# Banks emptied by ScalarE alone, memory values in rows of 512 columns, and transposes of x in pairs, in a two-layer decoder trunk

## The chip, the cores and the metric

The kernel runs on one core of one Trainium2 chip. The metric is the device time of one execution in microseconds (us), as the median of three runs. The engines are TensorE (PE, matmuls), VectorE (DVE), ScalarE (ACT), GpSimd (POOL) and SyncE (SP), which here issues the DMAs.

## What is computed

Two layers of a decoder trunk over 512 tokens of 1024 channels. Each layer projects x once, feeds four gated branches of width 512 (an RWKV-7 recurrence, latent attention, a convolution module, cross-attention into 256 memory tokens), merges them, projects, and normalises. Cut to what the change touches:

```python
h = x @ W_in                       # split among the branches
# B: latent attention, 8 heads
q = (rms_norm(q_lat, q_norm) @ w_uq).reshape(B, S, H, 96)
kv = (rms_norm(kv_lat, kv_norm) @ w_ukv).reshape(B, S, H, 128)
# C: convolution module
y = depthwise_conv31(a * sigmoid(b)); y = silu(layer_norm(y))
# M: cross-attention into the memory
k, v = split(mem @ w_mem_kv)       # 256 memory tokens, 512 columns each
# end of a layer
x = layer_norm(alpha * x + merged @ w_out)
```

## The kernel before

All large matmuls are in float32 accuracy, made of three products: each operand is split into a rounded high part `h` and a rest `lo` (`split`: ScalarE copies to `h`, VectorE subtracts to get `lo`), and `mm3` issues three matmuls per 128 rows. Activations lie with channels on the partitions, 512 tokens in the columns; a PSUM bank holds 128 x 512 values.

Weights stream through SBUF: SyncE loads one raw block of 512 KB after the other into two buffers, each is split (`w25h`, `w25l` and so on, numbered in the order of use), and the split parts have three buffers. `stream` takes the work items in order and prefetches up to four blocks.

The order of the instructions on each engine is fixed when the program is built. A class `Plan` runs the work items and side tasks as generators, keeps a modelled clock for every engine, and at each step lets the task go on whose inputs are due. `plan.due` tells it when a task's inputs are ready, `yield` hands over, `plan.spawn` starts a side task. So an edit in one task can move instructions of others.

PSUM has three pools. `pp` has two banks, used by every projection (`project`, through which also `pq`, `pk` of the attention heads, `ps_xq`, `ps_mk` pass, and the narrow items `pz`, `pmv`); `pa` has two, used by transposes and small products (`ct`, `cb` of the convolution, `xT` of x); `pg` has four.

Touched parts:

- `heads` takes a scaled projection bank (`pq` or `pk`, two heads) and makes the two parts `xqh`, `xql` (or `xkh`, `xkl`); DMAs then put them in place. ScalarE and VectorE both read the bank.
- `conv_norm` transposes the convolution's result (`ct`), takes statistics and normalises into `cn`, and transposes back (`cb`), from where `ctn` (tanh) and `yc` (affine) are made.
- `memory_items` gives four key items (each 24 matmuls, bank `ps_mk`) and two value items (`vpart`, through `narrow`: two blocks of 128 x 256, bank `pmv`) per layer.
- At the end of layer 0, z (the sum before the last normalisation) comes from `out_item` (half z0) and quarter items (z2, z3). `norm` normalises the tokens; behind the fourth token block it transposes x for layer 1, `xT0` to `xT7`, one bank at a time, into `xf` and its parts `xh`, `xl`.
- `ORDER` (line 26) is the list, written by hand, in which those items and layer 1's memory items are put in the stream: m0 to m3 are keys, m4 and m5 values.

Of the kernel before, what the change touches and what calls it, by code (L numbers as in the profile page):

```python
# [10 lines left out]
F32 = mybir.dt.float32  # L11
F32R = mybir.dt.float32r
# [3 lines left out]
AF = mybir.ActivationFunctionType  # L16
ALU = mybir.AluOpType
# [5 lines left out]
SEQ = 512  # L23
DM = 1024
U_SLOTS = 32
ORDER = ["z0", "m0", "m1", "z2", "m2", "m4", "z3", "m3", "m5"]
LOOK = 4
GATHER = 1500.0
WR = 2
# [236 lines left out]
def trunk_kernel(ctx: ExitStack, tc: tile.TileContext, A, out, dbg=None):  # L266
    nc = tc.nc
    plan = Plan(tc.keep_in_program_order)
# [19 lines left out]
    def TR(o, i):  # L288
        plan.shape(128, 128)
        plan.op("PE", 109.0, _names(o), _names(i))  # L290
        plan.keep(nc.tensor.transpose(o, i, ident))  # L291
# [12 lines left out]
    xp = pool(8, name="xp")  # L304
# [194 lines left out]
    def wide(get, ps, lhs, wait=None):  # L499

        for k in range(8):
            h, lo = yield from get()
            if wait:
                yield from wait(k)
            for b in range(len(ps)):
                xh, xl = lhs(k, b)
                mm3(ps[b], xh, xl, h, lo, k == 0, k == 7)
                if b % 2 and (k < 7 or b < 3):
# [34 lines left out]
    closed = [False] * LAYERS  # L543
# [8 lines left out]
    def close_phase():  # L552
        phase[0].close()

    def memory_items(l):

        ms = []
        res = {}

        def load(pool):  # L560
            raws = []
            for i in range(4):
                raws.append(u(f"mr{i}_{l}"))
# [12 lines left out]
        def keep(x, i, b, ps):  # L576
            h, lo = (y[:, 256 * b:256 * b + 256] for y in res[x][i])
            return split(h, lo, ps)

        def keys(h):  # L580
            def run(get):
                ps = yield from project(get, ms, f"mk{h}_{l}", 256)
                yield from keep("k", h // 2, h % 2, ps)
                yield
            return run

        def vpart(b):
            def after(i, ps):
                yield from keep("v", i, b, ps)
                if b == i == 1:  # L590
                    MEM[l] = (res["k"], res["v"])
                yield

            def run(get):
                return narrow(get, 256, 2, f"pmv{b}{l}", lambda k, i: [x[:, 128 * i:128 * i + 128] for x in ms[k]], after)
            return run

        its = [([(A["w_mk"][l, h], (512, 512))], keys(h)) for h in range(4)]
        its += [([(A["w_mv"][l, b, kh], (512, 512)) for kh in range(2)], vpart(b)) for b in range(2)]
        return load, its, lambda: len(ms) == 8  # L600

    def layer_items(l):
# [4 lines left out]
        def pr(n, i=0, w=1):  # L607
            return PRM[l][0][:, PCOL[n] + i:PCOL[n] + i + w]
# [540 lines left out]
        def conv_norm():  # L1149
            ntok = []  # L1150
            yield lambda: added[3] == 8
            for tb in range(4):
                ps, = yield from pa.take([128, 512], f"ct{tb}" + t_)
                for i in range(4):
                    TR(ps[:, 128 * i:128 * i + 128], cacc[i][:, 128 * tb:128 * tb + 128])
                yield
                bs, mv = st(f"cbs{tb}" + t_, 6), st(f"cmv{tb}" + t_, 2)
                V.bn_stats(bs, ps)
                V.bn_aggr(mv, bs)
                rs = st(f"crs{tb}" + t_, 1)  # L1160
                rstd_of(rs, mv[:, 1:2], 1.0, LN_EPS)
                n = u(f"cn{tb}" + t_)
                V.tensor_scalar(out=n, in0=ps, scalar1=mv[:, 0:1], scalar2=rs, op0=ALU.subtract, op1=ALU.mult)
                pa.free()
                ntok.append(n)
                yield
            yield lambda: added[1] >= 4
            for i in range(4):
                ps, = yield from pa.take([128, 512], f"cb{i}" + t_)
                plan.due(*ntok)  # L1170
                yield "pe"
                for tb in range(4):
                    TR(ps[:, 128 * tb:128 * tb + 128], ntok[tb][:, 128 * i:128 * i + 128])
                yield
# [458 lines left out]
        def end_items():  # L1633
# [148 lines left out]
            def norm(tb):  # L1782
# [29 lines left out]
                if E["n"] < 4:  # L1812
                    return
                for k in range(8):
                    ps, = yield from pa.take([128, 512], f"xT{k}" + t_)
                    plan.due(*[z[tb][k // 4] for tb in range(4)])
                    yield
                    for tb in range(4):
                        TR(ps[:, 128 * tb:128 * tb + 128], z[tb][k // 4][:, 128 * (k % 4):128 * (k % 4) + 128])
                    yield  # L1820
                    f = u(f"xf{k}" + t_)
                    h = xp.tile([128, 512], F32R, tag="xh", name=f"xh{k}_{l + 1}")
                    lo = xp.tile([128, 512], F32R, tag="xl", name=f"xl{k}_{l + 1}")
                    S.activation(f, ps, AF.Identity, scale=pr("ln_g", k), bias=pr("ln_b", k))
                    pa.free()
                    S.copy(h, f)
                    V.tensor_tensor(out=lo, in0=f, in1=h.bitcast(F32), op=ALU.subtract)
                    X[l + 1].append((h, lo))
                close_phase()
                closed[l] = True  # L1830

            if l + 1 < LAYERS:
                load, its, there = memory_items(l + 1)
# [135 lines left out]
def layout(x, mem, positions, w_in, b_gate, rwkv_mu, rwkv_w0, rwkv_w2, rwkv_a0, rwkv_a2, rwkv_k_k, rwkv_k_a,  # L1969
# [30 lines left out]
    a["w_mv"] = np.stack([tiles(xattn_w_mem_kv[l][:, 512:], 256, 4) for l in range(L)])  # L2000
# [35 lines left out]
```

## Time and profile before

| | |
|---|---|
| median of 3 runs | 1505.58 us (1505.47 to 1506.05) |
| profiled execution | 1506.66 us |
| its span | 1504.9 us |
| mean granted TensorE clock | 0.996 |
| busy: PE, PE weight load, DVE, ACT, POOL | 1474.2, 1239.7, 1053.5, 662.1, 137.1 us |
| matmuls | 11896 |

The profiler takes one execution; its own time is 1.8 us more than its span. Busy time is that in which the engine executes; matmuls are pipelined, so a busy TensorE may still be waited on. A row such as `PE pq L286 <- DVE xql L235` says that a matmul into `pq` waited for VectorE's `xql`. L235 and L286 are helper lines, which all operations of an engine share, so that names of tiles and not lines tell the operations apart.

### The profile page before, as it was taken

The page shows a single profiled execution, that of the slowest core. Times are in us where ns is not written, and L with a number is a line of the kernel's source. Part 1 is how long each engine was busy: PE and PEld are TensorE (multiplying, and loading weights), DVE is VectorE, ACT ScalarE, POOL GpSimd, SP SyncE. Part 2 cuts the span into 40 slices and gives each one's busy share as a digit, 9 for nine tenths or more (in the row PEclk, how much of TensorE's full clock was granted, in tenths as well). Part 3 has the DMA queues.
Part 4 walks back from the last instruction along what each step waited for, and adds up shares of the span by engine and source line. Part 5 has one row for each costly group of instructions (what it writes and reads, how often), then busy time and mean ns, then how long its engine had stood idle before and what let it go on. Part 6 is the DMA issues. An engine that isn't in the chain of part 4 may idle for free.

```text
span 1504.9 us, 29132 instructions
## 1 busy us (share of the span) xinstructions
PE 1474.2 (98%) x11896; PEld 1239.7 (82%) x11896; DVE 1053.5 (70%) x1994; ACT 662.1 (44%) x1270; POOL 137.1 (9%) x329
## 2 busy tenths in 40 slices
PE   8999999999999999999999999999999999999997
PEld 8888878888888888888998878888887788888886
DVE  5799997755757666645554888887876476757747
ACT  5546554434354543443255455533444344444332
POOL 0000000030303030000010000000030203021002
PEclk9999999999999999999999999999999999999998
DMA  6444333241322323434343252423332313233532
GB/s 213 124 136 108 86 100 96 84 111 59 86 83 78 91 74 95 136 103 129 114 147 108 82 138 68 116 92 99 88 95 72 97 47 107 63 107 116 165 99 70
DMA packets 89013, 153.50 MB, mean 102 GB/s; under 512 B 41008, under 2 KB 47152, under 8 KB 88880
## 3 DMA queue, kind: packets, MB, share of 16 engines
q1 hardware_dynamic: 88880, 151.65, 33.9%
q8 instruction: 93, 1.52, 0.4%
q14 instruction: 40, 0.33, 0.1%
HBM read 134.32 MB, written 5.77 MB: 93 GB/s over the span
## 4 chain that ended last, share of the span: by engine, by line
PE 90%; DVE 5%; ACT 2%; issue 1%; DMA 1%; POOL 0%; SPq 0%; ACTq 0%; POOLq 0%; DVEq 0%
PE ps_m L286 23%; PE po L286 11%; PE ps_xq L286 3%; PE ps_v L286 3%; PE ps_xg L286 3%; PE ps_cg L286 3%; PE ps_rg L286 3%; PE ps_k L286 3%; PE ps_mg L286 3%; PE ps_r L286 3%; PE ps_val L286 3%; PE ps_glu L286 2%; PE ms L286 2%; PE pl L286 2%; PE pz L286 2%; PE pmv L286 2%
## 5 line engine op out<-in xcount | busy, mean ns | idle before, releaser
L235 DVE SCALAR_TENSOR_TENSOR cacc<-hpad,prm,cacc 128x512 f32<-128x512 f32 x240 | 179.2, 749 | 3.9
L235 ACT ACTIVATE tm<-ps_m,prm 128x512 f32<-128x512 f32 x64 | 44.1, 689 | 166.6 <-PE ps_m L286 156.1
L235 DVE SCALAR_TENSOR_TENSOR mt<-tm,po 128x512 f32<-128x512 f32 x48 | 32.9, 686 | 89.9 <-PE po L286 89.6
L235 POOL TENSOR_TENSOR tmpW<-ZT,W 64x14 f32<-64x14 f32 (+6 forms) x112 | 42.7, 381 | 7.8
L235 POOL TENSOR_TENSOR ZT<-ZT,tmpW 64x14 f32<-64x14 f32 (+6 forms) x112 | 42.0, 375 | 8.8
L235 ACT ACTIVATE mP<-ms,nmm 128x128 f32<-128x128 f32 (+3 forms) x64 | 33.6, 529 | 20.3 <-DVE nmm L235 19.5
L235 POOL TENSOR_SCALAR ZT<-W 64x256 f32<-64x256 f32 x8 | 3.6, 447 | 369.7 <-DMA W<-scr 369.7
L235 ACT COPY mPT<-mt 128x128 f32<-128x128 f32 (+3 forms) x64 | 26.1, 428 | 19.6 <-PE mt L291 19.4
L235 DVE TENSOR_TENSOR merged<-merged,mt 128x512 f32<-128x512 f32 x48 | 33.6, 699 | 1.7
L235 POOL MEMSET D<- 128x8 f32 x8 | 0.9, 116 | 342.7 <-PE ms L286 321.2
L235 DVE TENSOR_REDUCE nmm<-ms 128x1 f32<-128x128 f32 (+3 forms) x64 | 30.0, 484 | 0.1
L235 POOL TENSOR_SCALAR lrs<-lmv 128x1 f32<-128x1 f32 x8 | 3.6, 447 | 253.6 <-DVE lmv L235 252.2
L235 DVE TENSOR_SCALAR mP<-mP,smm 128x128 f32<-128x128 f32 (+3 forms) x64 | 24.8, 387 | 2.3
L291 PE MATMUL mt<-cst,mP 128*128 128x128 f32 x160 | 25.9, 273 | 0.0
L235 DVE SCALAR_TENSOR_TENSOR merged<-tm,po 128x512 f32<-128x512 f32 x16 | 11.0, 687 | 20.1 <-PE po L286 20.0
L235 ACT ACTIVATE z<-z,lnb,lrs 128x256 f32<-128x256 f32 (+1 forms) x16 | 9.6, 647 | 30.1 <-DVE lnb L235 30.1
L235 POOL TENSOR_SCALAR gr<-gm 128x8 f32<-128x8 f32 x8 | 2.4, 298 | 224.0 <-DVE gm L235 224.0
L235 ACT ACTIVATE yb<-yb,mr,gr 128x64 f32<-128x64 f32 x64 | 22.1, 434 | 1.1 <-DVE mr L235 1.1
L286 PE MATMUL ms<-kTl,qT 96*128 96x128 f32 (+3 forms) x64 | 22.3, 348 | 0.0
L291 PEld LDWEIGHTS mt<-cst,mP 128*128 128x128 f32 x160 | 19.0, 141 | 3.6 <-ACT xP L235 0.2
L235 ACT ACTIVATE xP<-xs,nmx 128x256 f32<-128x256 f32 x32 | 15.1, 473 | 13.7 <-DVE nmx L235 11.2
L286 PE MATMUL ms<-kTh,qT 96*128 96x128 f32 (+3 forms) x64 | 20.6, 322 | 0.0
(3536 smaller groups left out, 5276.3 us busy)
## 6 DMA issues: line engine op xcount, KB each, us to landing
w<-in_w_ch_dram SPq DMA_DIRECT2D x146, 512.0 KB, 3.8
w<-in_w_o_dram SPq DMA_DIRECT2D x32, 512.0 KB, 3.7
w<-in_w_out_dram SPq DMA_DIRECT2D x16, 512.0 KB, 3.7
w<-in_w_lat_dram SPq DMA_DIRECT2D x16, 336.0 KB, 3.2
w<-in_w_mk_dram SPq DMA_DIRECT2D x8, 512.0 KB, 3.7
w<-in_w_mv_dram SPq DMA_DIRECT2D x8, 512.0 KB, 3.7
w<-in_w_qk_dram SPq DMA_DIRECT2D x8, 320.0 KB, 2.9
x<-in_xT_dram SPq DMA_DIRECT2D x8, 256.0 KB, 5.9
```

Source lines behind the costliest of these rows:

```text
L235: return self.plan.keep(f(*a, **k))
L286: plan.keep(nc.tensor.matmul(o, lhsT, rhs, start=start, stop=stop))
L291: plan.keep(nc.tensor.transpose(o, i, ident))
```

## The change

Four edits:

1. In `heads` ScalarE copies the scaled bank to SBUF (in the tile of `lo`), and `split` makes both parts from there; VectorE no longer reads the bank. Eight copies more a layer on ScalarE.
2. In `conv_norm` ScalarE copies `ct` to SBUF and the bank is free; statistics and normalisation read the copy. The affine part of `yc` goes from VectorE to ScalarE.
3. A layer's memory values are one item through `wide`, with 48 matmuls of 512 columns in place of 96 of 256. In layer 1 it takes both `pp` banks, in layer 0 one `pp` and one `pa`. The weights `w_mv` are laid out for it, and in `ORDER` all of it stands behind z3 and m3, while before m4 stood ahead of z3.
4. The transposes of x are eight side tasks (`features`), so that both `pa` banks are in use at once.

```diff
-ORDER = ["z0", "m0", "m1", "z2", "m2", "m4", "z3", "m3", "m5"]
+ORDER = ["z0", "m0", "m1", "z2", "m2", "z3", "m3", "m4"]
...
-        def vpart(b):
-            def after(i, ps):
-                yield from keep("v", i, b, ps)
...
-                return narrow(get, 256, 2, f"pmv{b}{l}", lambda k, i: [x[:, 128 * i:128 * i + 128] for x in ms[k]], after)
+        def values(get):
+            ps = [pp.tile([128, 512], F32, tag="pp", name=f"pmv{i}_{l}") for i in range(1 + (l > 0))]
+            if l == 0:
+                ps += yield from pa.take([128, 512], f"pmv1_{l}")
+            yield from wide(get, ps, lambda k, b: [x[:, 128 * b:128 * b + 128] for x in ms[k]])
...
+            plan.spawn(after())
...
-        its += [([(A["w_mv"][l, b, kh], (512, 512)) for kh in range(2)], vpart(b)) for b in range(2)]
+        its += [([(A["w_mv"][l, i], (512, 512)) for i in range(4)], values)]
...
+                n = u(f"cn{tb}" + t_)
+                S.copy(n, ps)
+                pa.free()
                 bs, mv = st(f"cbs{tb}" + t_, 6), st(f"cmv{tb}" + t_, 2)
-                V.bn_stats(bs, ps)
+                V.bn_stats(bs, n)
...
-                V.tensor_scalar(out=n, in0=ps, scalar1=mv[:, 0:1], scalar2=rs, op0=ALU.subtract, op1=ALU.mult)
-                pa.free()
+                plan.due(rs)
+                yield
+                V.tensor_scalar(out=n, in0=n, scalar1=mv[:, 0:1], scalar2=rs, op0=ALU.subtract, op1=ALU.mult)
...
-                V.tensor_scalar(out=z, in0=ps, scalar1=pr("cln_g", i), scalar2=pr("cln_b", i), op0=ALU.mult, op1=ALU.add)
+                S.activation(z, ps, AF.Identity, scale=pr("cln_g", i), bias=pr("cln_b", i))
...
-            S.activation(parts[0], ps, AF.Copy, scale=s)
-            V.scalar_tensor_tensor(out=parts[1], in0=ps, scalar=s, in1=parts[0].bitcast(F32), op0=ALU.mult, op1=ALU.subtract)
+            raw = parts[1].bitcast(F32)
+            S.activation(raw, ps, AF.Copy, scale=s)
+            yield from split(*parts, raw)
...
                 for k in range(8):
-                    ps, = yield from pa.take([128, 512], f"xT{k}" + t_)
...
+                    plan.spawn(features(k, [z[tb][k // 4][:, 128 * (k % 4):128 * (k % 4) + 128] for tb in range(4)]))
```

What it does to the order. First, ScalarE in layer 0, at the first two pairs of attention heads (`pq`, `pk` are banks, `w25h` a weight's high part, `ps_xq` the bank of the projection that follows). Before:

```order
L235 COPY w25h<-w_1193 128x1024
L235 ACTIVATE xqh_1223<-pq_0_1203 128x512
L235 ACTIVATE xkh_1232<-pk_0_1219 128x512
L235 COPY w26h<-w_1230 128x1024
L235 ACTIVATE xqh_1272<-pq_0_1244 128x512
L235 ACTIVATE xkh_1283<-pk_0_1268 128x512
L235 ACTIVATE xqh_0_1324<-ps_xq_0_1280 128x512
```

After:

```order
L235 COPY w25h<-w_1139 128x1024
L235 ACTIVATE xql_1169<-pq_0_1149 128x512
L235 COPY xqh_1168<-xql_1169 128x512
L235 ACTIVATE xkl_1180<-pk_0_1164 128x512
L235 COPY xkh_1179<-xkl_1180 128x512
L235 ACTIVATE xql_1213<-pq_0_1191 128x512
L235 COPY xqh_1212<-xql_1213 128x512
L235 COPY w26h<-w_1177 128x1024
L235 ACTIVATE xkl_1234<-pk_0_1208 128x512
L235 COPY xkh_1233<-xkl_1234 128x512
L235 ACTIVATE xqh_0_1274<-ps_xq_0_1230 128x512
```

Each bank is read by one ScalarE instruction, `xql` or `xkl`, which writes the raw values; the high part is a second copy from SBUF behind it.

Second, TensorE at the end of layer 0, where layer 1's keys (`ps_mk`), its values (`pmv`) and the transposes of x (`xT`) meet. Before:

```order
L286 MATMUL ps_mk_1_8406<-memh_1_7798,w124l 128x256
L286 MATMUL pmv_8443<-w125l,memh_1_7792 128x256
L286 MATMUL pmv_8443<-w125h,memh_1_7792 128x256
L286 MATMUL pmv_8443<-w125h,meml_1_7793 128x256
...
L291 MATMUL xT_0_8434<-cst,z_0_7314 128x128
L286 MATMUL pmv_8443<-w125l,memh_1_7794 128x256
...
L291 MATMUL xT_0_8464<-cst,z_0_7314 128x128
L286 MATMUL pmv_8443<-w126l,memh_1_7796 128x256
```

After:

```order
L286 MATMUL ps_mk_1_8298<-memh_1_7756,w122l 128x256
L286 MATMUL pmv_1_8334<-w123l,memh_1_7750 128x512
L286 MATMUL pmv_1_8334<-w123h,memh_1_7750 128x512
L286 MATMUL pmv_1_8334<-w123h,meml_1_7751 128x512
L286 MATMUL pmv_1_8335<-w123l,memh_1_7750 128x512
...
L291 MATMUL xT_0_8344<-cst,z_0_7272 128x128
L291 MATMUL xT_0_8345<-cst,z_0_7266 128x128
...
L291 MATMUL xT_0_8345<-cst,z_0_7272 128x128
L286 MATMUL pmv_1_8334<-w123l,memh_1_7750 128x512
```

The second bank of the values is opened at once, and two groups of transposes stand side by side; before, one group stood between pieces of six value matmuls.

ScalarE at the same place (`z` is the normalisation of the last token block, `kmh` the high part of the keys, `xf` and `xh` what is made of a transposed bank). Before:

```order
L235 ACTIVATE z_0_7314<-z_0_7314,lnb_0_8430,lrs_0_8400 128x512
L235 COPY kmh_1_7802<-ps_mk_1_8406 128x256
L235 ACTIVATE xf_0_8458<-xT_0_8434,prm_194 128x512
L235 COPY xh_1_8459<-xf_0_8458 128x512
L235 COPY w126h<-w_8407 128x1024
L235 ACTIVATE xf_0_8479<-xT_0_8464,prm_194 128x512
```

After:

```order
L235 ACTIVATE z_0_7272<-z_0_7272,lnb_0_8322,lrs_0_8292 128x512
L235 COPY kmh_1_7760<-ps_mk_1_8298 128x256
L235 COPY w124h<-w_8299 128x1024
L235 ACTIVATE xf_0_8359<-xT_0_8344,prm_194 128x512
L235 COPY xh_1_8360<-xf_0_8359 128x512
L235 ACTIVATE xf_0_8364<-xT_0_8345,prm_194 128x512
```

The split of the values' next weight now stands ahead of the first copy out of the transposes. SyncE issues that weight's load, in both programs, behind the four stores of `xtok`.

Third, ScalarE in layer 1, at the first two pairs of heads (`yxg0h` and `xP` belong to the cross-attention). Before:

```order
L235 COPY w147h<-w_9552 128x1024
L235 ACTIVATE xqh_9585<-pq_1_9565 128x512
L235 COPY w148h<-w_9602 128x1024
L235 ACTIVATE xkh_9607<-pk_1_9581 128x512
L235 COPY yxg0h_9623<-xy_1_9266 128x512
L235 ACTIVATE xP_1_9589,smx_1_9597<-xs_1_9578,nmx_1_9596 128x256
L235 ACTIVATE xqh_9653<-pq_1_9619 128x512
```

After:

```order
L235 ACTIVATE xql_9490<-pq_1_9469 128x512
L235 COPY xqh_9489<-xql_9490 128x512
L235 COPY w148h<-w_9507 128x1024
L235 ACTIVATE xkl_9513<-pk_1_9485 128x512
L235 COPY xkh_9512<-xkl_9513 128x512
L235 COPY yxg0h_9528<-xy_1_9170 128x512
L235 ACTIVATE xP_1_9493,smx_1_9502<-xs_1_9482,nmx_1_9501 128x256
L235 ACTIVATE xql_9549<-pq_1_9524 128x512
```

Two copies more stand between the readings of the two `pq` banks.

More of the change, by code (lines that the diff above doesn't have):

```diff
@@ L507, in wide @@
                 mm3(ps[b], xh, xl, h, lo, k == 0, k == 7)
-                if b % 2 and (k < 7 or b < 3):
+                if b % 2 and (k < 7 or b < len(ps) - 1):
                     yield
@@ L574, in load, with keep @@
                     ms.append((h[:, c], lo[:, c]))
-        def keep(x, i, b, ps):
-            h, lo = (y[:, 256 * b:256 * b + 256] for y in res[x][i])
+        def keep(x, i, c, ps):
+            h, lo = (y[:, c] for y in res[x][i])
             return split(h, lo, ps)
@@ L582, in run, with after @@
                 ps = yield from project(get, ms, f"mk{h}_{l}", 256)
-                yield from keep("k", h // 2, h % 2, ps)
+                yield from keep("k", h // 2, slice(256 * (h % 2), 256 * (h % 2) + 256), ps)
                 yield
             return run
-        def vpart(b):
-            def after(i, ps):
-                yield from keep("v", i, b, ps)
[L590 to L594, printed above, removed]
-                return narrow(get, 256, 2, f"pmv{b}{l}", lambda k, i: [x[:, 128 * i:128 * i + 128] for x in ms[k]], after)
-            return run
+        def values(get):
[3 more added lines that the diff above has]
+            yield from wide(get, ps, lambda k, b: [x[:, 128 * b:128 * b + 128] for x in ms[k]])
+            def after():
+                for i in range(2):
+                    yield from keep("v", i, slice(0, 512), ps[i])
+                if l == 0:
+                    pa.free()
+                MEM[l] = (res["k"], res["v"])
+            plan.spawn(after())
+            yield
         its = [([(A["w_mk"][l, h], (512, 512))], keys(h)) for h in range(4)]
-        its += [([(A["w_mv"][l, b, kh], (512, 512)) for kh in range(2)], vpart(b)) for b in range(2)]
+        its += [([(A["w_mv"][l, i], (512, 512)) for i in range(4)], values)]
         return load, its, lambda: len(ms) == 8
@@ L1156, in conv_norm @@
                 yield
+                n = u(f"cn{tb}" + t_)
+                S.copy(n, ps)
+                pa.free()
                 bs, mv = st(f"cbs{tb}" + t_, 6), st(f"cmv{tb}" + t_, 2)
-                V.bn_stats(bs, ps)
+                V.bn_stats(bs, n)
                 V.bn_aggr(mv, bs)
@@ L1161, in conv_norm @@
                 rstd_of(rs, mv[:, 1:2], 1.0, LN_EPS)
-                n = u(f"cn{tb}" + t_)
-                V.tensor_scalar(out=n, in0=ps, scalar1=mv[:, 0:1], scalar2=rs, op0=ALU.subtract, op1=ALU.mult)
-                pa.free()
+                plan.due(rs)
+                yield
+                V.tensor_scalar(out=n, in0=n, scalar1=mv[:, 0:1], scalar2=rs, op0=ALU.subtract, op1=ALU.mult)
                 ntok.append(n)
@@ L1814, in norm, with features @@
                 for k in range(8):
-                    ps, = yield from pa.take([128, 512], f"xT{k}" + t_)
[L1816 to L1830, printed above, removed]
+                    plan.spawn(features(k, [z[tb][k // 4][:, 128 * (k % 4):128 * (k % 4) + 128] for tb in range(4)]))
+            def features(k, zs):
+                ps, = yield from pa.take([128, 512], f"xT{k}" + t_)
+                plan.due(*zs)
+                yield
+                for tb in range(4):
+                    TR(ps[:, 128 * tb:128 * tb + 128], zs[tb])
+                yield
+                f = u(f"xf{k}" + t_)
+                h = xp.tile([128, 512], F32R, tag="xh", name=f"xh{k}_{l + 1}")
+                lo = xp.tile([128, 512], F32R, tag="xl", name=f"xl{k}_{l + 1}")
+                S.activation(f, ps, AF.Identity, scale=pr("ln_g", k), bias=pr("ln_b", k))
+                pa.free()
+                yield from split(h, lo, f)
+                while len(X[l + 1]) < k:
+                    yield lambda: len(X[l + 1]) == k
+                X[l + 1].append((h, lo))
+                if k == 7:
+                    close_phase()
+                    closed[l] = True
             if l + 1 < LAYERS:
@@ L1999, in layout @@
     a["w_mk"] = np.stack([tiles(xattn_w_mem_kv[l][:, :512], 128, 8)[:, 0] for l in range(L)])
-    a["w_mv"] = np.stack([tiles(xattn_w_mem_kv[l][:, 512:], 256, 4) for l in range(L)])
+    a["w_mv"] = np.stack([tiles(xattn_w_mem_kv[l][:, 512:], 512, 2)[0] for l in range(L)])
     a["w_o"] = np.stack([[tiles(w_o_branch[l, n], 128, 4)[:, 0].reshape(4, 2, 128, 512).transpose(0, 2, 1, 3).reshape(4, 128, 1024)
```

## The prediction

> **What bounds the kernel now.** I read the page first, then the chain of waits, then TensorE's own waits, and last the timelines around each wait that the change could touch.
>
> ```profile
> PE 1474.2 (98%) x11896; PEld 1239.7 (82%) x11896; DVE 1053.5 (70%) x1994; ACT 662.1 (44%) x1270; POOL 137.1 (9%) x329
> PE 90%; DVE 5%; ACT 2%; issue 1%; DMA 1%; POOL 0%; SPq 0%; ACTq 0%; POOLq 0%; DVEq 0%
> ```
>
> TensorE (PE) is busy for 1474.2 of a span of 1504.9 us and carries 90% of the chain that ends last; VectorE (DVE) follows with 5%, ScalarE (ACT) with 2%. So an instruction taken from VectorE or given to ScalarE counts only where a matmul waits for it. TensorE's list of waits names those places, in us in total, number of times and the longest:
>
> ```profile
> PE pl L286 <- DVE w0l L235: 6.7, 1, 6.7
> PE pmv L286 <- DVE w126l L235: 2.6, 1, 2.6
> PE tk L291 <- DVE S L235: 1.8, 1, 1.8
> PE pq L286 <- DVE xql L235: 1.6, 2, 0.9
> PE ps_xq L286 <- DVE xql L235: 1.4, 2, 0.9
> PE ps_glu L286 <- DVE xql L235: 1.1, 1, 1.1
> PE gb_0x L286 <- issue: 1.1, 1, 1.1
> PE ps_mg L286 <- DVE xql L235: 0.6, 1, 0.6
> PE gb_1x L286 <- issue: 0.6, 1, 0.6
> PE pz L286 <- DVE w123l L235: 0.6, 1, 0.6
> ```
>
> The 6.7 us are the start, which the change leaves alone. Six waits, in four rows, are for `xql`, the part that VectorE makes out of a projection bank in `heads`: 1.6 + 1.4 + 1.1 + 0.6 = 4.7 us. One of 2.6 us is for a weight of the memory values. No row names a bank of the convolution's transposes (`ct`, `cb`), and none names ScalarE. These are what the change can win; the rest must come from fewer matmul starts. What a start costs is read from undisturbed runs of matmuls in the chain (start, length, what):
>
> ```profile
> 64.86 5.47 PE ps_glu L286 x24
> 86.49 11.53 PE pmv L286 x96
> 740.55 2.88 PE ps_mk L286 x24
> ```
>
> A projection's 24 matmuls of 512 columns take 5.47 us, 0.228 each; 96 of 256 columns take 11.53, 0.120 each.
>
> **The attention heads: who empties the bank.** The timeline of layer 0's first pair (start, duration, engine; the wait before it in brackets):
>
> ```profile
> 105.80 0.59 ACT L235 ACTIVATE xqh<-pq 128x512 fp32r<-128x512 f32 x1
> 105.93 1.22 DVE L235 TENSOR_TENSOR w25l<-w,w25h 128x1024 fp32r<-128x1024 f32 x1 [0.45 <-ACT w25h L235]
> 106.52 0.39 PE L286 MATMUL pk<-lth,w23l 128*128 128x512 f32 x1
> 107.07 0.68 DVE L235 SCALAR_TENSOR_TENSOR xql<-pq,xqh 128x512 fp32r<-128x512 f32 x1
> 107.81 0.50 PE L286 MATMUL pq<-ltl,w24h 128*128 128x512 f32 x1 [0.90 <-DVE xql L235]
> 108.15 0.39 PE L286 MATMUL pq<-lth,w24h 128*128 128x512 f32 x1
> ```
>
> ScalarE has read `pq` by 106.39. VectorE still has to, and stands behind a weight's `w25l` until 107.07. TensorE, ready at about 106.52 + 0.23 = 106.75, starts at 107.81. So the whole loss is 1.06 us, not 0.90, and the next start comes 0.34 later in place of 0.23: one such stop costs 0.27 more than its bracket. Six of them: 4.7 + 6 x 0.27 = 6.3 us. After the change one ScalarE copy frees the bank, and `h` and `lo` are made from SBUF. In this place that is at 106.39, ahead of 106.75: no stop. The copies that are added (16 in all, `xqh` and `xkh`) delay only the head's parts, which TensorE needs after the next pair's projections.
>
> The places in layer 1 are tighter, as the rows there show:
>
> ```profile
> 877.63 1.04 ACT L235 CAST w148h<-w 128x1024 fp32r<-128x1024 f32 x1 [1.31 <-PE pk L286]
> 878.52 0.50 PE L286 MATMUL pq<-ltl,w146h 128*128 128x512 f32 x1 [0.75 <-DVE xql L235]
> 879.07 0.61 ACT L235 CAST yxg0h<-xy 128x512 fp32r<-128x512 f32 x1
> 879.58 0.48 ACT L235 ACTIVATE xP<-xs,nmx 128x256 f32<-128x256 f32 x1
> ```
>
> ScalarE's order after the change puts six instructions between the first pair's copy and the second's: `xqh`, `w148h`, the copy of `pk`, `xkh`, `yxg0h`, `xP`, and only then the copy of `pq`. By these durations (0.6, 1.04, 0.6, 0.6, 0.61, 0.48, 0.6) its end comes some 0.7 us after TensorE wants the bank. So I leave one stop of 0.7 + 0.27 there: 6.3 - 1.0 = 5.3 us gained. The ends are 3.0 (half of the six stops come back as waits for ScalarE's copies) and 6.3.
>
> The Trainium skill, "VectorE: DVE Perf Modes", Rules for kernel authors, advises for work on matmul output either to take the slower PSUM read or to copy to SBUF first if many operations follow. Only two operations follow here, so by that rule the copy does not pay, and the sum would be the second rival's -3.3. The trace shows, in the 0.90 us row above, a queue ahead of the read as the cost, which the rule does not weigh.
>
> **The memory values: half the matmuls, twice the rows.** A layer's 96 matmuls of 256 columns take 11.53 us. After the change 48 of 512 columns do the same: 48 x 0.228 = 10.94. That is 0.6 less per layer, 1.2 in both.
>
> **The layer boundary.** Before, `pmv` is made of two items, the second half behind z3 and m3; after, all of it stands behind them, between the eight groups of transposes of x.
>
> ```profile
> 761.40 0.28 PE L286 MATMUL ps_mk<-meml,w124h 128*128 128x256 f32 x1
> 764.77 0.81 ACT L235 ACTIVATE z<-z,lnb,lrs 128x512 f32<-128x512 f32 x1 [2.33 <-DVE lnb L235]
> 765.49 0.35 ACT L235 CAST kmh<-ps_mk 128x256 fp32r<-128x256 f32 x1
> 765.87 0.42 DVE L235 TENSOR_TENSOR kml<-ps_mk,kmh 128x256 fp32r<-128x256 f32 x1 [0.68 <-ACT kmh L235]
> 766.51 0.60 PE L291 MATMUL xT<-cst,z 128*128 128x128 f32 x4
> 768.40 1.23 DVE L235 TENSOR_TENSOR w126l<-w,w126h 128x1024 fp32r<-128x1024 f32 x1 [0.25 <-ACT w126h L235]
> 769.68 2.75 PE pmv L286 x12
> ```
>
> Removed: the wait of 2.6 us for `w126l` (TensorE now has nine long matmuls and twelve transposes behind that point before it needs the second value weight), the 0.6 us wait of `pz` for `w123l` (the key item m2 now stands between z2 and z3, so the weight has longer), twice 0.27 for restarting, and a slow stretch behind the long wait: its 12 matmuls take 2.75 us where 12 x 0.12 = 1.44 is usual, 1.3 lost. Sum 2.6 + 0.6 + 0.5 + 1.3 = 5.0.
>
> Added: the values now hold both projection banks, and the second is the one `ps_mk` has just left. The first three wide matmuls can start at 761.40 + 2.88 = 764.28 and end at 764.96. The next three need the bank of `ps_mk`, which VectorE's `kml` holds until 765.87 + 0.42 = 766.29, since `kmh` stands behind the normalisation `z` on ScalarE: 766.29 - 764.96 = 1.3, and 0.27 for the restart. The values' second weight comes from a DMA that stands behind the four stores of `xtok` on SyncE's queue, as before:
>
> ```profile
> 761.95 0.46 SPq L298 DMA_DIRECT2D w<-in_w_mv_dram  x1
> w<-in_w_mv_dram SPq DMA_DIRECT2D x1, 512.0 KB, 4.5
> ```
>
> It lands at 761.95 + 4.5 = 766.45. ScalarE now splits it straight away (1.04), ahead of the first copy out of the transposes (`w124h` ahead of `xf`), and VectorE adds 1.23, so it is ready by about 768.7. TensorE, from 766.3 + 0.27 on, has nine wide matmuls (2.05) and three groups of four transposes (0.60 each) ahead of it, to about 770.4: not late. The transposes' banks come free later by ScalarE's order, for which I allow 0.3. Added: 1.3 + 0.27 + 0.3 = 1.9. Net: 5.0 - 1.9 = 3.1 gained.
>
> **Convolution.** `ct` leaves its bank by a ScalarE copy and is read from SBUF; the `yc` affine goes from VectorE to ScalarE.
>
> ```profile
> L235 DVE TENSOR_SCALAR yc<-cb,prm x8: 804/810/812, 462.0 to 1211.1; 128x512 f32<-128x512 f32 x8
> L235 ACT ACTIVATE xf<-xT,prm x8: 771/778/781, 766.0 to 789.5; 128x512 f32<-128x512 f32 x8
> 139.20 0.59 ACT L235 COPY mo<-mo 128x512 f32<-128x512 f32 x1 [1.32 <-PE mo L286]
> ```
>
> ScalarE gains 8 x 0.59 and 8 x 0.78 us, VectorE loses 8 x 0.81 (its `cn` stays, from SBUF). No matmul waits for either bank now, so I count nothing: TensorE's queue of other branches' matmuls covers it. Without that cover it would cost the 20.3 us of the third rival.
>
> **Layer 0's middle.** The planner puts the matmuls of layer 0's attention and RWKV stretch in another order; layer 1's repeats the old pattern. What such a stretch can cost is read from the waits that stand in layer 1's: 1.8 + 1.1 + 0.6 = 3.5 (`tk` and the two `gb`) if they appear in layer 0 too. At the other end nothing: layer 0's stretch has no wait of this size in the list, so there is none to win. I take +1.0, nearer to nothing because in the old order layer 0 has none of the three.
>
> **The sum.** -5.3 - 1.2 - 3.1 + 1.0 = -8.6. The profiled execution took 1506.66 us: 1498.1 after. It lies 1.1 above the median of 1505.58, within 0.1%; from the median, 1497.0. A change within 0.2% (3.0 us) is one that a measurement of this kernel can hardly tell from none.
>
> **The rivals.** *The slow stretch at the boundary comes back (0.15).* The windows show that TensorE's clock was halved behind the 2.57 us wait, and not behind another of 1.75 us (start and end, length, TensorE busy and count, granted clock, DMA share, GB/s):
>
> ```profile
> 770.00:771.00 1.00, 1.00 (x7) 0.50 0.50 75
> 1200.00:1202.00 2.00, 2.00 (x76) 1.00 0.58 147
> 1198.82 0.63 PE L291 MATMUL tk<-cst,v 128*128 128x128 f32 x4 [1.75 <-DVE S L235]
> ```
>
> After the change a wait of 1.3 us and two groups of transposes stand close together there. If they count together as idleness, the 1.3 us lost to the slow stretch stay, and about 1.0 more since twice as many columns run in it: 2.3, 1499.3 us. The Trainium skill, "TensorE: Matmul & The Clock Gate", What's actually happening, gives an idle window of about 3.4 us for the throttle, and Part 4 says transposes do not count as busy; the trace agrees in that the 2.57 us wait behind four transposes halved the clock.
>
> *The heads' copy gains little (0.12).* The bank is freed by ScalarE, but its copy then stands as far back in ScalarE's queue as VectorE's read stood in its own, as in layer 1's second pair. Only what is left without that term: -1.2 - 3.1 + 1.0 = -3.3, 1502.3 us. Against it: ScalarE is busy 44%, VectorE 70%.
>
> *ScalarE becomes late (slower, 0.10).* Every added ScalarE instruction is waited for: 16 x 0.59 + 8 x 0.59 + 8 x 0.78 = 20.3 us on TensorE's path, -8.6 + 20.3 = +11.7, 1517.3 us. It turns the result slower from 8.6 of 20.3, 42%, on that path; with the 3.0 us of the limit, from 57%. Against it: no wait of TensorE names ScalarE now.
>
> *The new order gives it back (0.08).* If layer 0 gets the 3.5 us of layer 1's waits, the boundary gains nothing (a new wait for a value weight in place of the old), and the heads give the low end of 3.0: -3.0 - 1.2 + 3.5 = -0.7, 1504.9 us, no change to be told.
>
> **How the numbers follow.** The forecast has 0.55, 1497.0 us. Its own ends: 1492.5 with all six stops gone, no wait at `kml` and no loss in the middle; 1500 with 3.0 from the heads and half the rest. The range goes to 1503.5 to take in the first two rivals and most of the last. Faster by over 0.2% (below 1502.6): the forecast, the first rival and half of the second, 0.76; within: the other half and the last, 0.14; slower 0.10, the ScalarE rival.
>
> **What would show it.** Right: TensorE's waits without `pq`, `ps_xq`, `ps_glu`, `ps_mg` for `xql` except one of some 0.7 us in layer 1; 48 `pmv` matmuls a layer in 10.9 us; no wait of `pmv` for a weight, but one of about 1.3 for `kml`; a clock of 1.00 around the boundary; ScalarE's busy time up by some 20 us. `tk`'s 1.8 us in layer 1 stays, since that stretch is not re-ordered. Wrong: waits that name ScalarE's copies of `pq`, `pk`, `ct` or `yc`; half clock behind the transposes; new waits in layer 0 of more than 4 us in sum.

## The result and the profile after

The changed kernel takes 1494.05 us (median of four, 1492.67 to 1496.11), the kernel before 1505.53 (1505.01 to 1506.05): a ratio of 0.9925, 95% interval 0.9908 to 0.9942, 11.5 us less. Forecast were 1497.0 and 8.6 less, with a range of 1492.5 to 1503.5. The profiled execution is the slowest of the four, 1496.11 us, with a span of 1494.2.

The page after, engines and chain:

```profile
PE 1470.5 (98%) x11800; PEld 1232.5 (82%) x11800; DVE 1045.0 (70%) x1982; ACT 678.6 (45%) x1298; POOL 141.3 (9%) x329
PE 91%; DVE 5%; ACT 2%; DMA 1%; issue 1%; POOL 0%; SPq 0%; ACTq 0%; DVEq 0%; POOLq 0%
```

TensorE carries the chain as before, with 96 matmuls fewer; ScalarE is busy 16.5 us more (20 were reckoned). TensorE's list of waits after:

```profile
PE pl L286 <- DVE w0l L235: 6.7, 1, 6.7
PE tk L291 <- DVE S L235: 1.6, 1, 1.6
PE pmv L286 <- DVE kml L235: 1.2, 1, 1.2
PE pq L286 <- ACT xql L235: 0.8, 1, 0.8
PE po L286 <- DVE merged L235: 0.8, 1, 0.8
PE ps_rg L286 <- issue: 0.5, 1, 0.5
```

The four rows for VectorE's `xql` are gone, and with them `w126l`, `w123l` and both `gb`. New are `kml`, 1.2 us, and one wait for ScalarE's `xql`, 0.8, at layer 0's first `pq`, where the raw weight came later and ScalarE's copy stood behind the weight's split. At the boundary the timeline reads:

```profile
755.87 0.39 PE L286 MATMUL pmv<-w123h,meml 128*128 128x512 f32 x1
757.46 0.50 PE L286 MATMUL pmv<-w123l,memh 128*128 128x512 f32 x1 [1.20 <-DVE kml L235]
758.26 1.03 PE L291 MATMUL xT<-cst,z 128*128 128x128 f32 x8
760.88 0.48 PE L286 MATMUL pmv<-w124l,memh 128*128 128x512 f32 x1
```

The rows between are left out. Three wide matmuls, the bank wait (1.3 had been worked out), three more, eight transposes in a row, six matmuls and four transposes more, and then the second weight `w124l` without a wait. The windows behind it (start and end, length, TensorE busy and count, granted clock, DMA share, GB/s) have the full clock, where before it was halved:

```profile
758.00:760.00 2.00, 2.00 (x14) 1.00 1.00 385
760.00:762.00 2.00, 2.00 (x12) 1.00 0.82 253
```

To see where the time went, the starts of matmuls that both programs have in the same place were compared in the two traces. The values of layer 0 stand between these:

```profile
86.33 0.28 PE L286 MATMUL pmv<-w18l,memh 128*128 128x256 f32 x1
97.84 0.40 PE L286 MATMUL ps_glu<-xl,w22h 128*128 128x512 f32 x1
```

and after:

```profile
86.19 0.40 PE L286 MATMUL pmv<-w18l,memh 128*128 128x512 f32 x1
97.10 0.39 PE L286 MATMUL ps_glu<-xl,w22h 128*128 128x512 f32 x1
```

That is 11.51 and 10.91 us: the 0.6 of the forecast. In the same way for whole stretches, each from its first matmul to that of the next, with one execution of each kernel:

| stretch | gain, us |
|---|---|
| layer 0 up to the third `ps_glu`, values included | 0.7 |
| layer 0 from there to the first `pz` | 1.5 |
| from there to layer 1's first `ps_glu` (boundary, with layer 1's values) | 4.5 |
| layer 1's attention, to `ps_wlal` | 1.3 |
| layer 1's recurrence, to `ps_rg` | 3.4 |
| the rest | -0.7 |

The boundary is near its forecast (3.1 + 0.6). But layer 0's middle and layer 1's attention give less together, 2.8, than the heads alone were to bring, 5.3, and the recurrence gives 3.4 where nothing was forecast. (The traced execution is the slowest of the four. In the traces of experiments 1 and 3 to 8, whose TensorE order in layer 1's attention is the same as the changed kernel's, that stretch gains 2.1 to 2.2 and not 1.3.) The right sum may have the wrong terms. So the edits were taken apart.

### The profile page after: what moved, and what is told of

Same layout as the page of the kernel before. It is cut to its first block, busy times and chain, and to the rows that moved or that the text cites. A ratio compares the mean times of both kernels' runs of the same rounds, so it can differ in the third digit from the quotient of the medians.

```text
span 1494.2 us, 28950 instructions
## 1 busy us (share of the span) xinstructions
PE 1470.5 (98%) x11800; PEld 1232.5 (82%) x11800; DVE 1045.0 (70%) x1982; ACT 678.6 (45%) x1298; POOL 141.3 (9%) x329
## 4 chain that ended last, share of the span: by engine, by line
PE 91%; DVE 5%; ACT 2%; DMA 1%; issue 1%; POOL 0%; SPq 0%; ACTq 0%; DVEq 0%; POOLq 0%
PE ps_m L286 24%; PE po L286 12%; PE ps_v L286 3%; PE ps_cg L286 3%; PE ps_rg L286 3%; PE ps_xq L286 3%; PE ps_k L286 3%; PE ps_r L286 3%; PE ps_mg L286 3%; PE ps_val L286 3%; PE ps_xg L286 3%; PE ps_glu L286 2%; PE pz L286 2%; PE pl L286 2%; PE ms L286 2%; PE x L286 2%
## 5 line engine op out<-in xcount | busy, mean ns | idle before, releaser
L235 DVE SCALAR_TENSOR_TENSOR cacc<-hpad,prm,cacc 128x512 f32<-128x512 f32 x240 | 179.1, 749 | 4.0
L235 ACT ACTIVATE tm<-ps_m,prm 128x512 f32<-128x512 f32 x64 | 44.1, 688 | 160.8 <-PE ps_m L286 140.0
L235 DVE SCALAR_TENSOR_TENSOR mt<-tm,po 128x512 f32<-128x512 f32 x48 | 32.9, 686 | 91.2 <-PE po L286 91.1
L235 ACT ACTIVATE mP<-ms,nmm 128x128 f32<-128x128 f32 (+3 forms) x64 | 33.8, 529 | 22.2 <-DVE nmm L235 17.2
L235 POOL TENSOR_TENSOR tmpW<-ZT,W 64x14 f32<-64x14 f32 (+6 forms) x112 | 41.9, 375 | 8.0
L235 POOL TENSOR_TENSOR ZT<-ZT,tmpW 64x14 f32<-64x14 f32 (+6 forms) x112 | 39.2, 350 | 8.8
L235 POOL TENSOR_SCALAR ZT<-W 64x256 f32<-64x256 f32 x8 | 5.8, 721 | 354.9 <-DMA W<-scr 196.1
L235 DVE TENSOR_TENSOR merged<-merged,mt 128x512 f32<-128x512 f32 x48 | 33.3, 694 | 1.6
L235 ACT COPY mPT<-mt 128x128 f32<-128x128 f32 (+3 forms) x64 | 26.8, 426 | 14.5 <-PE mt L291 13.5
L235 POOL MEMSET D<- 128x8 f32 x8 | 0.9, 116 | 334.3 <-PE ms L286 318.3
L235 DVE TENSOR_REDUCE nmm<-ms 128x1 f32<-128x128 f32 (+3 forms) x64 | 30.8, 485 | 0.1
L235 DVE SCALAR_TENSOR_TENSOR merged<-tm,po 128x512 f32<-128x512 f32 x16 | 11.0, 684 | 25.9 <-PE po L286 25.7
L235 POOL TENSOR_SCALAR lrs<-lmv 128x1 f32<-128x1 f32 x8 | 3.6, 447 | 254.1 <-DVE lmv L235 252.7
L235 DVE TENSOR_SCALAR mP<-mP,smm 128x128 f32<-128x128 f32 (+3 forms) x64 | 24.8, 387 | 2.3
L235 POOL TENSOR_SCALAR gr<-gm 128x8 f32<-128x8 f32 x8 | 3.7, 462 | 230.4 <-DVE gm L235 230.4
L235 ACT ACTIVATE z<-z,lnb,lrs 128x256 f32<-128x256 f32 (+1 forms) x16 | 9.6, 647 | 30.5 <-DVE lnb L235 30.5
L235 ACT ACTIVATE yb<-yb,mr,gr 128x64 f32<-128x64 f32 x64 | 22.1, 431 | 2.4 <-DVE mr L235 2.4
L286 PE MATMUL ms<-kTl,qT 96*128 96x128 f32 (+3 forms) x64 | 22.0, 344 | 0.0
L235 ACT ACTIVATE xP<-xs,nmx 128x256 f32<-128x256 f32 x32 | 15.2, 476 | 12.1 <-DVE nmx L235 11.6
L286 PE MATMUL ms<-kTh,qT 96*128 96x128 f32 (+3 forms) x64 | 20.6, 322 | 0.0
```

Source lines behind the costliest of these rows:

```text
L235: return self.plan.keep(f(*a, **k))
L286: plan.keep(nc.tensor.matmul(o, lhsT, rhs, start=start, stop=stop))
```

## The experiments

Times are medians; each ratio is against runs of the kernel before on the same chip. Those runs have medians from 1505.39 to 1505.91, so a difference between two experiments is safer by their ratios. A stretch of a trace is one execution: the first 97 us, with the same order on TensorE, took 96.1 to 97.4 us in the executions of the changed kernel and the experiments that share it.

**1. The heads alone** (the three lines in `heads`, nothing else).

> The kernel before with the edit of the heads alone. Theory A (a bank that one ScalarE copy frees): the six waits of TensorE for xql go, except one of 0.8 us for xql at the first pq of layer 0, as in the trace after; some 3 us in layer 0 and 2 in layer 1 are gained, and the re-ordered stretches of recurrence and attention move the rest by 1 to 2 either way: about -4, 1501.5 us. Theory B (the edit gains nothing, the gain of the change is elsewhere): within 1 us of 1505.5. Theory C (the edit also carries the 3.4 us that layer 1's recurrence lost in the trace after): -6 to -7, 1499 us.

1504.46 us, ratio 0.9993 (0.9984 to 1.0002): no gain that can be told. The time is theory B's; theory A fails, though its waits did go. From the list of waits:

```profile
PE ps_r L286 <- DVE mt L235: 2.9, 1, 2.9
PE pmv L286 <- DVE w126l L235: 2.6, 1, 2.6
PE ps_xq L286 <- ACT xql L235: 0.9, 1, 0.9
```

All six stops for VectorE's `xql` are gone, one of 0.9 for ScalarE's has come, and there is a new wait of 2.9 us in layer 0, of `ps_r` for `mt`. `mt` is VectorE's merge, which reads the bank of `po`; `ps_r` needs that bank. The windows behind it:

```profile
394.00:396.00 2.00, 1.09 (x5) 1.00 0.64 184
396.00:398.00 2.00, 2.00 (x7) 0.60 0.44 174
398.00:400.00 2.00, 2.00 (x6) 0.55 0.42 106
```

After the wait the clock falls to 0.60 and 0.55 for 4 us, another 1.7 lost. The stops removed in layer 0 are paid back in one place. In layer 1's attention, where no such wait came, the heads gained 2.2 us up to `ps_wlal`; its two stops were 0.75 + 0.86 + 2 x 0.27 = 2.15.

**2. Values, ORDER and paired transposes, without heads and convolution.**

> The kernel before with the values in rows of 512, the new ORDER and the paired transposes; heads and convolution as before. Theory A: -4.5 at the boundary and -0.6 in layer 0 as in the landmarks of the trace after, about -5.1, 1500.4 us; the six waits for xql stay (4.7 us), the half clock behind the boundary is gone. Rival: the boundary's gain needs the earlier shift by the heads (weights arrive relatively later), then the wait for a value weight stays and it is -1.2 to -2.5, 1503.5 us.

1501.51 us, ratio 0.9972 (0.9963 to 0.9981): 3.9 less, nearer to theory A than to its rival. In its trace the boundary stretch gains 4.5 us, as in the changed kernel, and the values of layer 0 gain 0.6. The stops for `xql` stay. So the boundary does not need the heads. The trace gains 3.8 us in all: 1.3 are lost behind layer 1's `ps_rg`, and some 1.7 behind layer 1's `tk`, where this execution's clock was halved.

**3. The convolution's edits undone**, the rest as changed.

> The changed kernel with the convolution's two edits undone. Theory A (they are free): within 1 us of 1494.0. Rival D (they carry the 3.4 us that layer 1's recurrence lost between the two traces, by freeing the transposes' banks sooner): 1497.4 us, with gb waits in layer 1 again. Rival E (the added ScalarE work costs and is hidden in the sum): 1 to 4 us faster than 1494.

1500.7 us, ratio 0.9967 (0.9955 to 0.9978): 6.6 slower than the changed kernel (6.3 by the two ratios). None of the three expectations holds in size. Its list of waits has `PE ps_r L286 <- DVE mt L235` with 2.9 us again. Values, transposes and heads together give 4.7 of the 11.5 us, as much as experiments 1 and 2 added (0.9 + 3.9); the convolution's edits, which I had counted at nothing, give the rest. VectorE's timeline in this run, at the place of the wait:

```profile
389.84 1.22 DVE L235 TENSOR_TENSOR w65l<-w,w65h 128x1024 fp32r<-128x1024 f32 x1
390.98 0.69 DVE L235 BATCH_NORM_STATS2 cbs<-ct 128x6 f32<-128x512 f32 x1
391.70 0.18 DVE L235 BATCH_NORM_AGGREGATE cmv<-cbs 128x2 f32<-128x6 f32 x1
392.83 0.81 DVE L235 TENSOR_SCALAR cn<-ct,cmv,crs 128x512 f32<-128x512 f32 x1 [0.94 <-POOL crs L235]
393.55 0.68 DVE L235 SCALAR_TENSOR_TENSOR mt<-tm,po 128x512 f32<-128x512 f32 x1
```

TensorE's last `po` matmul ends at 391.4, and the next projection wants the bank; `mt`, which would free it, stands behind a weight's split, the statistics of `ct`, and `cn`, which sits 0.94 us waiting for GpSimd's `crs`. In the changed kernel:

```profile
389.48 0.69 DVE L235 SCALAR_TENSOR_TENSOR mt<-tm,po 128x512 f32<-128x512 f32 x1 [1.23 <-PE po L286]
390.21 0.69 DVE L235 TENSOR_TENSOR merged<-merged,mt 128x512 f32<-128x512 f32 x1
390.81 1.22 DVE L235 TENSOR_TENSOR w65l<-w,w65h 128x1024 fp32r<-128x1024 f32 x1
391.95 0.63 DVE L235 TENSOR_SCALAR cn<-cn,cmv,crs 128x512 f32<-128x512 f32 x1
392.50 0.67 DVE L235 SCALAR_TENSOR_TENSOR mt<-tm,po 128x512 f32<-128x512 f32 x1
```

Here `mt` stands first and waits for TensorE, not the other way round, and `cn` comes when `crs` has long been there. In the kernel before, `cn` also sat idle for `crs` (all eight `cn` did, 7.9 us together), but it stood well ahead of the end of `po`, and the weight's split stood behind `mt`:

```profile
389.87 0.81 DVE L235 TENSOR_SCALAR cn<-ct,cmv,crs 128x512 f32<-128x512 f32 x1 [0.94 <-POOL crs L235]
392.12 0.69 DVE L235 SCALAR_TENSOR_TENSOR mt<-tm,po 128x512 f32<-128x512 f32 x1 [1.44 <-PE po L286]
393.45 1.22 DVE L235 TENSOR_TENSOR w65l<-w,w65h 128x1024 fp32r<-128x1024 f32 x1
```

So the idle time was there before, and only the new order put it in front of TensorE. Two lines of the convolution's edit take it away from this place: `plan.due(rs)` and `yield` between the statistics and `cn`. In this profiled execution the clock stayed full behind the wait; it is the fastest of its six, 1498.3 us, so its trace shows the 2.9 us of the wait and not the slow stretch behind it that experiment 1's trace has. Experiments 5 and 6 take the two lines apart from the copies.

**4. m3 ahead of z3.**

```diff
-ORDER = ["z0", "m0", "m1", "z2", "m2", "z3", "m3", "m4"]
+ORDER = ["z0", "m0", "m1", "z2", "m2", "m3", "z3", "m4"]
```

> The changed kernel with the last key item m3 ahead of z3, so that its bank is empty long before the values ask for both. Theory A (the 1.2 us wait of pmv for kml is a bank wait, and the values alone cover the last normalisation): the wait goes, -1.2 and 0.3 for the restart, 1492.5 us. Rival: the normalisation of the last token block now has 2.9 us less work behind it, and TensorE waits that much for it or for a value weight: 1494 to 1496 us.

1493.8 us, ratio 0.9923 (0.9911 to 0.9936): the same as the changed kernel. The wait for `kml` is gone, and one of the same size is there: `pz` for `w122l`, behind two key items in a row, each of which uses up a weight in 2.9 us.

```profile
PE pz L286 <- DVE w122l L235: 1.2, 1, 1.2
```

**5. The two lines alone, without ScalarE's copies.**

```diff
                 rstd_of(rs, mv[:, 1:2], 1.0, LN_EPS)
+                plan.due(rs)
+                yield
                 n = u(f"cn{tb}" + t_)
```

> The kernel without the convolution's edits (heads, values, transposes changed), with two of their lines put back: behind the statistics of a transposed block, the task says when the reciprocal deviation crs is due and hands over, so that VectorE does other work before the normalisation cn; the bank is still read and held by VectorE. Theory A (the 6.6 us are this: cn no longer stands in VectorE's queue waiting for crs, with the merge mt behind it whose bank TensorE wants): the 2.9 us wait of ps_r for mt is gone and the time is that of the changed kernel, 1494 us. Rival B (the gain is that ScalarE frees the bank, or that cn and yc cost VectorE less): 1500 us, as without the edits.

1496.72 us, ratio 0.9937 (0.9923 to 0.9951). The wait of `ps_r` is gone, as theory A had it, and 4.0 of the 6.6 us are there (4.5 of 6.3 by the ratios). `mt` at that place again waits for TensorE:

```profile
388.48 0.69 DVE L235 SCALAR_TENSOR_TENSOR mt<-tm,po 128x512 f32<-128x512 f32 x1 [0.72 <-PE po L286]
```

**6. ScalarE's copies without the two lines.**

> The changed kernel without those two lines: ScalarE's copy of ct and its yc stay, but VectorE's cn follows the statistics at once. Theory A: the wait of ps_r for mt of about 2.9 us is back and the time is 1499 to 1501 us. Rival B: 1494 us.

1497.42 us, ratio 0.9938 (0.9925 to 0.9950). The wait is there, but shorter:

```profile
PE ps_r L286 <- DVE mt L235: 2.1, 1, 2.1
```

VectorE's queue has the same order as in experiment 3, and `cn` waits for `crs` as there, but it reads SBUF and is 0.26 us shorter (0.55 for 0.81), and VectorE comes to `w65l` 0.55 us earlier against the end of `po`:

```profile
391.37 0.55 DVE L235 TENSOR_SCALAR cn<-cn,cmv,crs 128x512 f32<-128x512 f32 x1 [0.94 <-POOL crs L235]
391.83 0.68 DVE L235 SCALAR_TENSOR_TENSOR mt<-tm,po 128x512 f32<-128x512 f32 x1
```

So each half of the convolution's edit brings a part, 4.0 and 3.3 by the medians (4.5 and 4.4 by the ratios), and both together 6.6 (6.3). In part they shorten the same wait: against experiment 3's trace, layer 0's middle is 2.9 us shorter with the lines, 2.1 with the copies and 2.9 with both. The copies also act elsewhere: layer 1's recurrence is 1.1 us shorter with them and 1.4 with both, and only 0.1 with the lines alone. In experiment 6 neither theory's time came. The intervals of experiments 5 and 6 overlap each other's and the changed kernel's, so the split between the two halves is rough.

**7. Heads and the two lines**, on the kernel before.

> The kernel before with the heads' edit and the same two lines, nothing else. Theory A (the heads' edit is worth its stops, but the order that it brings has put cn ahead of mt): -0.9 of the heads alone becomes -0.9 - 5 to 6.6, that is 1498 to 1499.5 us. Rival (the heads' edit is worth 1 us whatever stands around it, and the two lines help only with the values' new order): 1503 to 1504.5 us.

1500.01 us, ratio 0.9959 (0.9946 to 0.9971), against 0.9993 for the heads alone. Theory A's range is missed by half a microsecond; the rival falls. No wait for `xql` or `mt` is left in its list.

**8. The key items spread.**

```diff
+ORDER = ["m0", "z0", "m1", "m2", "z2", "m3", "z3", "m4"]
```

> The changed kernel with ORDER m0 z0 m1 m2 z2 m3 z3 m4: m3 ahead of z3 as before, but never two key items right before z3, so that the weight w122l of z3 has a whole z2 item and one key item to arrive. Theory A (the 1.2 us wait moved from kml to w122l because two key items take their weights in 2.9 us each): neither wait, 1492.5 us. Rival: the values' weights or the normalisation are late then: 1494 us, with a wait of 1 us or more in their name.

1493.93 us, ratio 0.9920 (0.9907 to 0.9934): again the same. Neither `kml` nor `w122l` is waited for; a wait of the transposes is there in their place:

```profile
PE xT L291 <- ACT xf L235: 1.6, 1, 1.6
```

The boundary has some 1.2 to 1.6 us that move from one wait to another as items are exchanged: the key bank, then a weight, then the transposes' banks.

**9. The two lines alone on the kernel before.**

> The kernel before with the two lines behind the statistics alone (VectorE's normalisation cn no longer follows the statistics at once). In the order of before no matmul waits for mt, so by theory A the lines find no wait to remove: within 1 us of 1505.5, and the heads' edit, beside the run of heads and these lines at 1500.0, is worth 5 us. By theory F (the lines help wherever they stand, the heads' edit gives 1 us in any order): 1500 to 1501 us.

1505.18 us, ratio 0.9997 (0.9988 to 1.0006): nothing, as theory A had it. Beside experiment 7 the heads' edit is worth 0.38% of 1505.5, 5.7 us (some 2 either way, by the two intervals), when VectorE's order does not take it back.

**10. Heads and the two lines, with the copy on VectorE.**

```diff
-            S.activation(raw, ps, AF.Copy, scale=s)
+            V.tensor_scalar(out=raw, in0=ps, scalar1=s, scalar2=None, op0=ALU.mult)
```

> The kernel before with the heads' edit and the two lines, but the copy out of the bank made by VectorE and not by ScalarE: still one reader of the bank, now in the queue in which the weights' low parts stand (a copy behind w25l and behind w147l in the order). Theory A (the queue ahead of the read is the cost): stops for VectorE's copies return in two to four places, 1502 to 1504.5 us. Theory G (one reader in place of two is what counts): 1500 us, as with ScalarE's copy.

1505.7 us, ratio 0.9999 (0.9990 to 1.0008): the whole gain is gone. One reader of the bank is not enough.

```profile
106.24 1.23 DVE L235 TENSOR_TENSOR w25l<-w,w25h 128x1024 fp32r<-128x1024 f32 x1 [1.07 <-ACT w25h L235]
107.38 0.68 DVE L235 TENSOR_SCALAR xql<-pq 128x512 f32<-128x512 f32 x1
108.12 0.50 PE L286 MATMUL pq<-ltl,w24h 128*128 128x512 f32 x1 [1.56 <-DVE xql L235]
```

The copy stands behind the split `w25l` on VectorE, and TensorE's stop is 1.56 us, more than the 0.90 of before. The stops for `xql` in its list come to 5.1 us, 4.7 before.

**11. The paired transposes alone, and 12. the values and ORDER alone**, on the kernel before.

> The kernel before with the paired transposes of x alone. Theory A (the boundary's gain comes from the order of the values, which puts nine long matmuls between the transposes and the second value weight): the wait for w126l stays, 2 to 3 us, with the half clock behind it; within 1 us of 1505.5. Rival (the transposes one at a time held TensorE up): -3 to -4, 1502 us.

> The kernel before with the values in rows of 512 and the new ORDER alone. Theory A: the whole gain of values and transposes together, about -4, 1501.5 us, with the wait of 1.2 us for kml. Rival (without pairs the transposes leave TensorE waiting between value matmuls): -1 to -2, 1504 us.

1504.62 us, ratio 0.9992 (0.9983 to 1.0001), and 1503.67, ratio 0.9986 (0.9977 to 0.9994). With the transposes alone the time is theory A's, but the wait for `w126l` went, against theory A, and `xT` waited 2.2 us for ScalarE's `xf` in its place. With the values alone, the time is the rival's, 1504; `kml` is waited for as theory A had it, but so are the weights:

```profile
PE pmv L286 <- DVE w124l L235: 1.6, 1, 1.6
PE pmv L286 <- DVE w126l L235: 0.5, 1, 0.5
```

The boundary stretch gains 1.5 us in the one trace and 2.3 in the other, 4.5 with both (experiment 2). But in both the clock stayed full there, and that alone is worth as much as the smaller gain: in experiment 10, where TensorE's order at the boundary is that of before and the wait for `w126l` is 2.57 us again, the clock stayed full too, and the stretch was 1.6 us shorter than before.

```profile
770.00:772.00 2.00, 1.64 (x13) 1.00 0.28 31
```

So at full clock the transposes alone gain nothing there, the values alone 0.7, and both 2.9. Both edits are needed. The waits fit with the reason that eight transposes in a row give the weight time, and that the long matmuls give ScalarE time to empty the transposes' banks.

## Why the prediction was right, and where it was not

**The heads, -5.3.** Right in mechanism and size, but not by itself. Run 10 shows that the queue ahead of the read is what costs; runs 7 and 9 give 5.7 us, some 2 either way, and layer 1's two stops 2.2. The stop expected at layer 1's second pair did not show; one of 0.8 at layer 0's first pair did. The second rival, that the copy brings nothing, falls with run 7, and with it the rule that counts the operations behind a copy: the same two follow in run 10, which gains nothing, and in run 7, which gains 5.7.

**Layer 0's middle, +1.0.** In the changed kernel this came near: by the rows of before the four stops of layer 0 were worth 0.90 + 0.57 + 0.64 + 1.14 + 4 x 0.27 = 4.3, one of 0.8 + 0.27 stayed, and the stretch gained 1.5, so 1.7 went to the new order (1.2 by experiment 8's trace, which has the same order there). But the reason was wrong. The order that the heads' edit brings costs 2.9 us and 1.7 of half clock in one place, 4.6, which is above the bound of 3.5 that was taken from other waits' sizes; run 1 ends at -0.9 for that. The changed kernel has no such wait because of the convolution's edits.

**The convolution, 0.** This is the step that failed. The reason given, that no matmul waits for `ct` or `cb`, was true of the trace of before and was not the question: the edits matter for what stands behind `cn` on VectorE. They are worth 6.6 us in the order that the heads bring (run 3), and their two lines nothing in the order of before (run 9); the copies were not run in that order. So heads and layer 0's middle, forecast together at -4.3, give -0.9 without the convolution's edits, these were forecast at 0 and give -6.6, and the sum of the two, -7.5 for -4.3, is 3.2 more than forecast; values and boundary take back 0.4 (run 2: -3.9 for -4.3). That the forecast is only some 2.9 short is luck in this part: an error of 3.4 one way and one of 6.6 the other.

**The values, -1.2.** Right: 0.60 measured in layer 0, where the stretch could be read by itself; layer 1's was not.

**The boundary, -3.1.** Right: 4.5 with layer 1's 0.6, so 3.9. The wait for `kml` was 1.20 for 1.3, no weight was late, and the clock stayed full, so the first rival did not come. The slow stretch, taken as 1.3, is worth 1.6 by run 10, and the 0.3 for the transposes' order was not seen.

**The rivals.** ScalarE's lateness did not come: it has 28 instructions more (32 added, and four fewer for the values), and one read of a head's bank is waited for, 0.8 us. The fourth, an order that gives it back, came in run 1, and the changed kernel escapes it by the convolution's edits.

**The range.** Its low end of 1492.5 does not come out of its own terms: 6.3 for the heads, 1.2, and 3.1 + 1.3 + 0.27 for the boundary are 12.2, which gives 1493.4. Nothing else hangs on it.

**Layer 1's recurrence, no term.** The prediction took this stretch as not re-ordered. It is: TensorE's order there differs between the two programs, its listed waits fall from 3.9 us to 1.6, and the stretch gains 3.4. The traces of runs 1, 3 and 5 gain 1.6, 2.1 and 2.2 us in it, those with ScalarE's copies (runs 4, 6 and 8) 3.1 to 3.6, so the copies have a part. The rest stays open: with TensorE's order of before the stretch still gains 0.8 in run 2, behind a halved clock, and waits named "issue" (1.7 us of `gb` before) come and go there. No version was measured that beats the changed kernel: runs 4 and 8 are the same within their intervals.

## What to carry to other kernels

When a bank is waited for, ask in which queue its reader stands: moving one copy from VectorE to ScalarE was worth 5.7 us, the same copy on VectorE nothing. When an edit moves instructions, look in the new order for a place where an instruction that waits for a third engine stands ahead of one that TensorE waits for. The trace of before shows only the first half of it: `cn` idle for `crs` eight times, and no matmul that waited. Edits that gain nothing alone can gain together, so a sum of separate terms may come out right by two errors.

## What the runs showed of the hardware

The same wait halves TensorE's clock in one execution and not in another. The 2.57 us for `w126l` did before and did not in experiment 10, with TensorE's order the same there. Behind 2.92 us of waiting for `mt` the clock fell to 0.60 in experiment 1; in experiment 3, behind 2.93 us, it stayed:

```profile
396.00:398.00 2.00, 2.00 (x10) 1.00 0.09 35
398.00:400.00 2.00, 2.00 (x10) 1.00 0.69 190
```

Even the 1.76 us wait of `tk` did so in two of the eight traces that have it, in experiment 2 here:

```profile
1192.00:1194.00 2.00, 0.75 (x5) 0.81 0.00 0
1194.00:1196.00 2.00, 2.00 (x7) 0.50 0.33 78
1196.00:1198.00 2.00, 2.00 (x75) 0.83 0.47 184
```

That wait stands between four transposes and four more, so between 1190.67 and 1193.99 no matmul but transposes started. By the granted shares the loss is the same in both places: 2 x (0.40 + 0.45) = 1.7 us in experiment 1, 2 x (0.19 + 0.50 + 0.17) = 1.7 in experiment 2.

The Trainium skill, "TensorE: Matmul & The Clock Gate", What's actually happening, calls the window of some 3.4 us free-running. That a wait halves the clock or not by where it falls agrees with it, but waits of 1.76 us are about half of the window.

The times of one kernel can go with it: in experiment 6 the two executions at a mean clock of 0.998 took 1494.7 and 1495.2 us, the three at 0.997 took 1497.4 to 1497.8. They do not always: in experiment 3, at 0.997, they run from 1498.3 to 1502.3. With 1.7 us lost behind it, a wait of 1.76 us costs up to about twice its length.
